# Rotary embedding on half the channels: from 2 MB tiles with 16 KB rows to 4 MB tiles with 32 KB rows, and another way to the tables

## The chip, the cores and the metric

The kernel runs on one core of a Trainium2 chip; the other cores are idle. The metric is the device time of one execution in microseconds (us), given as the median of several. Lower is better. A 'span' is the part of that time that the profiler records; here it is about 1.9 us shorter than the time. Sizes in MB follow the profile (33.55 MB is the whole of `x`); a '2 MB' tile has 2,097,152 bytes.

## The reference

```python
batch, seq, heads, dim = 16, 512, 16, 64          # x: float32, cos and sin: (512, 32)
x1, x2 = x[..., :32], x[..., 32:]
first  = x1[..., :16] * cos[..., :16] - x1[..., 16:] * sin[..., :16]
second = x1[..., :16] * sin[..., :16] + x1[..., 16:] * cos[..., :16]
out = concatenate([first, second, x2], axis=-1)
```

The second half of the channels only passes through. All of `x` (33.55 MB) is read and all of `out` is written, 67 MB in total, and there is little arithmetic for each byte.

## The kernel before

One batch entry is one tile: 512 sequence rows over 128 partitions, four rows per partition. Four rows of 16 heads x 64 floats are 16 KB, contiguous in memory. Loads go out on the sync queue (SP in the profile), stores on the scalar queue (ACT). VectorE (DVE) works in place on the tile. GpSimd (POOL) copies the two tables out to full size first.

```python
K = S // P                                  # 4 rows per partition: runs of 16 KB
xf = x.rearrange("b (p k) h d -> b p (k h d)", p=P)
x_pool = ctx.enter_context(tc.tile_pool(name="xp", bufs=6))
ab_pool = ctx.enter_context(tc.tile_pool(name="abp", bufs=4))
nc.gpsimd.dma_start(out=cosL[:], in_=cosf)
nc.gpsimd.dma_start(out=sinL[:], in_=sinf)
for k in range(K):                          # tables written out over heads and both halves
    nc.gpsimd.tensor_copy(out=dst_c, in_=src_c)
    nc.gpsimd.tensor_copy(out=dst_s, in_=src_s)
for b in range(B):                          # 16 tiles of 2 MB
    x_t = x_pool.tile([P, K, H, D], fp32)
    nc.sync.dma_start(out=x_t..., in_=xf[b])
    nc.vector.tensor_mul(out=a_t[:], in0=x12, in1=cc_op)      # 128 x 2048
    nc.vector.tensor_mul(out=b_t[:], in0=x12, in1=ss_op)
    nc.vector.tensor_tensor(out=x12[:, :, 0:Q], ..., op=subtract)   # 128 x 1024
    nc.vector.tensor_tensor(out=x12[:, :, Q:2*Q], ..., op=add)
    nc.scalar.dma_start(out=of[b], in_=x_t...)
```

## Time and profile before

| | before |
|---|---|
| time | 163.36 us median of 4 (163.12 to 163.46) |
| span | 161.4 us |
| bytes moved | 67.25 MB |
| VectorE busy | 67% |
| DMA, 50 to 141 us | 431 GB/s |

These are lines of the profile page of the kernel before. In the slices each digit is the busy share of 1/40 of the span, in tenths. A queue's line gives its packets, its MB and its share of the 16 DMA engines' time; q1 carries the loads, q10 the stores, q0 the tables. A line that begins with L64 stands for all instructions of line 64 of the kernel: output and inputs with their sizes, how many, then busy us and mean ns of one, then how long the engine was idle before them and what ended most of that wait.

```profile
span 161.4 us, 189 instructions
DVE 108.7 (67%) x64; POOL 6.0 (4%) x14
DMA  5999999999999999999999999999999999999994
...
q1 hardware_dynamic: 2304, 33.56, 49.4%
q10 hardware_dynamic: 2304, 33.56, 48.5%
q0 software_dynamic: 64, 0.13, 0.2%
...
L64 DVE TENSOR_TENSOR a_t<-x_t,CCX 128x2048 f32<-128x2048 f32 x16 | 37.0, 2313 | 42.1 <-DMA x_t<-in_x_dram 30.1
L66 DVE TENSOR_TENSOR x_t<-a_t,b_t 128x1024 f32<-128x1024 f32 x16 | 19.5, 1220 | 0.2
```

The DMA row is full from the second slice to the next to last, and the two tile queues fill 98% of the engines' time. VectorE is idle for a third of the span. It waits for loads; the loads themselves are late because the engines are full.

The table of stretches for the kernel before (start:end, length, busy time of DVE and of POOL with the number of instructions, clock, DMA share, GB/s) says it with a rate:

```profile
12.00:50.00 38.00, 37.83 (x22) 0.47 (x1) 1.00 1.01 426
50.00:141.00 91.00, 61.67 (x37) 0.00 (x0) 1.00 1.01 431
141.00:151.00 10.00, 9.12 (x6) 0.00 (x0) 1.00 1.01 434
151.00:161.40 10.40, 0.00 (x0) 0.00 (x0) 1.00 0.78 336
```

The next line is from the waits of the SP queue before (us in total, number of waits, the longest).

```profile
SPq L57 <- DMA out_dram<-x_t: 107.8, 10, 24.1
```

The load queue waits 107.8 us for stores to free a buffer. That looks like a shortage of buffers, but the engines never run empty meanwhile, and loads that were issued earlier are still moving: in the packet records the load queue has no gap longer than 0.2 us. So this wait costs nothing here.

### The profile page before, as it was taken

How to read it: one execution, taken by the hardware profiler on the slowest of the kernel's cores; microseconds unless marked ns; L12 is line 12 of the kernel's file. 1: busy time of each engine (PE TensorE's matmuls, PEld its weight loads, DVE VectorE, ACT ScalarE, POOL GpSimd, SP SyncE). 2: the span in 40 equal slices, each digit the busy share in tenths (PEclk: the TensorE clock that was granted, in tenths of full speed). 3: DMA queues.
4: the chain of work that ended last, by engine and by line, in shares of the span. 5: the costliest groups of instructions: out<-in, count | busy, mean ns of one | idle time of the engine just before them, and what ended most of it. 6: DMA issues, size and time to landing. Idle time of an engine off the chain costs nothing.

```text
span 161.4 us, 189 instructions
## 1 busy us (share of the span) xinstructions
DVE 108.7 (67%) x64; POOL 6.0 (4%) x14
## 2 busy tenths in 40 slices
DVE  0009999999995692947839296592957939389400
POOL 3090000000000000000000000000000000000000
DMA  5999999999999999999999999999999999999994
GB/s 162 430 414 447 414 382 443 414 430 447 418 434 434 422 443 430 418 451 422 426 443 422 430 434 430 434 434 418 447 422 426 451 414 428 439 422 438 430 422 195
DMA packets 4673, 67.25 MB, mean 417 GB/s; under 512 B 544, under 2 KB 544, under 8 KB 576
## 3 DMA queue, kind: packets, MB, share of 16 engines
q1 hardware_dynamic: 2304, 33.56, 49.4%
q10 hardware_dynamic: 2304, 33.56, 48.5%
q0 software_dynamic: 64, 0.13, 0.2%
q14 instruction: 1, 0.01, 0.0%
HBM read 33.69 MB, written 33.55 MB: 417 GB/s over the span
## 4 chain that ended last, share of the span: by engine, by line
DMA 60%; DVE 28%; POOL 2%; issue 2%; DVEq 1%; POOLq 0%; SPq 0%; PEldq 0%
DMA out_dram<-x_t 31%; DMA x_t<-in_x_dram 25%; DVE a_t L64 9%; DVE b_t L65 8%; DVE x_t L66 6%; DVE x_t L72 5%; DMA cosL<-in_cos_dram 4%; POOL CCX L49 1%; DVEq L105 1%; POOL SSX L50 1%; POOLq L105 0%; SPq L57 0%; DVEq L66 0%; PEldq L105 0%
## 5 line engine op out<-in xcount | busy, mean ns | idle before, releaser
L64 DVE TENSOR_TENSOR a_t<-x_t,CCX 128x2048 f32<-128x2048 f32 x16 | 37.0, 2313 | 42.1 <-DMA x_t<-in_x_dram 30.1
L65 DVE TENSOR_TENSOR b_t<-x_t,SSX 128x2048 f32<-128x2048 f32 x16 | 36.5, 2283 | 0.0
L66 DVE TENSOR_TENSOR x_t<-a_t,b_t 128x1024 f32<-128x1024 f32 x16 | 19.5, 1220 | 0.2
L72 DVE TENSOR_TENSOR x_t<-a_t,b_t 128x1024 f32<-128x1024 f32 x16 | 19.5, 1218 | 0.0
L49 POOL COPY CCX<-cosL 128x512 f32<-128x512 f32 x4 | 2.4, 612 | 5.4 <-DMA cosL<-in_cos_dram 5.4
L50 POOL COPY SSX<-sinL 128x512 f32<-128x512 f32 x4 | 2.4, 614 | 0.1
L39 POOL DMA_DIRECT2D cosL<-in_cos_dram x1 | 0.7, 668 | 0.8 <-PEq L105 0.8
L40 POOL DMA_DIRECT2D sinL<-in_sin_dram x1 | 0.5, 534 | 0.0
L94 POOL MEMSET const-float32-0.0<- 128x1 f32 x1 | 0.1, 98 | 0.2 <-issue 0.2
L94 POOL MEMSET const-bfloat16-1.0<- 128x1 bf16 x1 | 0.1, 101 | 0.0
L94 POOL MEMSET const-uint8-127<- 128x1 uint8 x1 | 0.1, 101 | 0.0
L94 POOL MEMSET const-float32-1.0<- 128x1 f32 x1 | 0.1, 98 | 0.0
## 6 DMA issues: line engine op xcount, KB each, us to landing
x_t<-in_x_dram SPq DMA_DIRECT2D x16, 2048.0 KB, 20.3
out_dram<-x_t ACTq DMA_DIRECT2D x16, 2048.0 KB, 23.4
cosL<-in_cos_dram POOLq DMA_DIRECT2D x1, 64.0 KB, 6.6
sinL<-in_sin_dram POOLq DMA_DIRECT2D x1, 64.0 KB, 7.1
```

Source lines behind the costliest of these rows:

```text
L39: nc.gpsimd.dma_start(out=cosL[:], in_=cosf)
L40: nc.gpsimd.dma_start(out=sinL[:], in_=sinf)
L49: nc.gpsimd.tensor_copy(out=dst_c, in_=src_c)
L50: nc.gpsimd.tensor_copy(out=dst_s, in_=src_s)
L64: nc.vector.tensor_mul(out=a_t[:], in0=x12, in1=cc_op)
L65: nc.vector.tensor_mul(out=b_t[:], in0=x12, in1=ss_op)
L66: nc.vector.tensor_tensor(out=x12[:, :, 0:Q], in0=a_t[:, :, 0:Q], in1=b_t[:, :, Q : 2 * Q], op=mybir.AluOpType.subtract,)
L72: nc.vector.tensor_tensor(out=x12[:, :, Q : 2 * Q], in0=a_t[:, :, Q : 2 * Q], in1=b_t[:, :, 0:Q], op=mybir.AluOpType.add,)
L94: nc = _bacc.Bacc("TRN2", target_bir_lowering=False, num_devices=1)
L105: with _tile.TileContext(nc) as tc:
```

## The change

The intent is larger transfers: eight rows per partition, so 32 KB runs and 4 MB tiles, eight tiles instead of sixteen, five buffers. A partition then holds eight consecutive rows, and two batch entries share a tile. The 512 rows of each table fill only 64 partitions, eight rows each; they are loaded there, and VectorE copies them into both halves of a 128-partition table. The tables are not written out over heads; the multiplies read them with a broadcast instead.

```diff
-    K = S // P
+    K = 8
+    T = B * S // (P * K)          # 8 tiles
+    PB = S // K                   # 64 partitions hold all table rows
...
-    x_pool = ctx.enter_context(tc.tile_pool(name="xp", bufs=6))
-    ab_pool = ctx.enter_context(tc.tile_pool(name="abp", bufs=4))
-    nc.gpsimd.dma_start(out=cosL[:], in_=cosf)
-    nc.gpsimd.dma_start(out=sinL[:], in_=sinf)
-    for k in range(K):  ... nc.gpsimd.tensor_copy x2
+    x_pool = ctx.enter_context(tc.tile_pool(name="xp", bufs=5))
+    ab_pool = ctx.enter_context(tc.tile_pool(name="abp", bufs=1))
+    stage = const_pool.tile([PB, 2, K, HF], fp32)
+    nc.scalar.dma_start(out=stage[:, 0]..., in_=cosf)
+    nc.scalar.dma_start(out=stage[:, 1]..., in_=sinf)
+    table = const_pool.tile([P, 2, K, 2, Q], fp32)
+    for r in range(2):
+        for t in range(2):
+            nc.vector.tensor_copy(out=table[r * PB : (r + 1) * PB, t], in_=stage[:, t, :, 0:Q]...broadcast)
...
+    for t in range(T):
+        nc.sync.dma_start(out=x_t..., in_=xf[t])          # 4 MB, 32 KB runs
+        for k0 in (0, 4):                                 # same VectorE shapes as before
+            ... two multiplies, subtract, add
+        nc.scalar.dma_start(out=of[t], in_=x_t...)
```

More of the change, by code (lines that the diff above doesn't have):

```diff
@@ L20 @@
     fp32 = mybir.dt.float32
+    P = 128
     B, S, H, D = x.shape
@@ L24 @@
     HF = D // 2
-    P = 128
-    K = S // P
-    xf = x.rearrange("b (p k) h d -> b p (k h d)", p=P)
-    of = out.rearrange("b (p k) h d -> b p (k h d)", p=P)
-    cosf = cos.rearrange("(p k) j -> p (k j)", p=P)
-    sinf = sin.rearrange("(p k) j -> p (k j)", p=P)
-    const_pool = ctx.enter_context(tc.tile_pool(name="const", bufs=1))
-    x_pool = ctx.enter_context(tc.tile_pool(name="xp", bufs=6))
-    ab_pool = ctx.enter_context(tc.tile_pool(name="abp", bufs=4))
-    cosL = const_pool.tile([P, K, HF], fp32)
@@ L38 @@
-    sinL = const_pool.tile([P, K, HF], fp32)
-    nc.gpsimd.dma_start(out=cosL[:], in_=cosf)
-    nc.gpsimd.dma_start(out=sinL[:], in_=sinf)
-    CCX = const_pool.tile([P, K, H, 2, Q], fp32)
-    SSX = const_pool.tile([P, K, H, 2, Q], fp32)
-    for k in range(K):
-        dst_c = CCX[:, k].rearrange("p h c j -> p (h c) j")
-        dst_s = SSX[:, k].rearrange("p h c j -> p (h c) j")
-        src_c = cosL[:, k : k + 1, 0:Q].to_broadcast((P, 2 * H, Q))
-        src_s = sinL[:, k : k + 1, 0:Q].to_broadcast((P, 2 * H, Q))
-        nc.gpsimd.tensor_copy(out=dst_c, in_=src_c)
-        nc.gpsimd.tensor_copy(out=dst_s, in_=src_s)
@@ L52 @@
-    cc_op = CCX.rearrange("p k h c j -> p (k h) (c j)")
-    ss_op = SSX.rearrange("p k h c j -> p (k h) (c j)")
-    for b in range(B):
-        x_t = x_pool.tile([P, K, H, D], fp32)
-        nc.sync.dma_start(out=x_t.rearrange("p k h d -> p (k h d)"), in_=xf[b])
-        a_t = ab_pool.tile([P, K * H, HF], fp32)
-        b_t = ab_pool.tile([P, K * H, HF], fp32)
-        x12 = x_t.rearrange("p k h d -> p (k h) d")[:, :, 0:HF]
-        nc.vector.tensor_mul(out=a_t[:], in0=x12, in1=cc_op)
-        nc.vector.tensor_mul(out=b_t[:], in0=x12, in1=ss_op)
-        nc.vector.tensor_tensor(
-            out=x12[:, :, 0:Q],
-            in0=a_t[:, :, 0:Q],
-            in1=b_t[:, :, Q : 2 * Q],
-            op=mybir.AluOpType.subtract,
-        )
-        nc.vector.tensor_tensor(
-            out=x12[:, :, Q : 2 * Q],
-            in0=a_t[:, :, Q : 2 * Q],
-            in1=b_t[:, :, 0:Q],
-            op=mybir.AluOpType.add,
-        )
-        nc.scalar.dma_start(out=of[b], in_=x_t.rearrange("p k h d -> p (k h d)"))
+    K = 8
@@ new lines @@
+    T = B * S // (P * K)
+    PB = S // K
+    REP = P // PB
+    xf = x.rearrange("b s h d -> (b s h d)").rearrange("(t p f) -> t p f", t=T, p=P)
+    of = out.rearrange("b s h d -> (b s h d)").rearrange("(t p f) -> t p f", t=T, p=P)
+    cosf = cos.rearrange("(p k) j -> p (k j)", k=K)
+    sinf = sin.rearrange("(p k) j -> p (k j)", k=K)
+    const_pool = ctx.enter_context(tc.tile_pool(name="const", bufs=1))
+    x_pool = ctx.enter_context(tc.tile_pool(name="xp", bufs=5))
+    ab_pool = ctx.enter_context(tc.tile_pool(name="abp", bufs=1))
@@ new lines @@
+    stage = const_pool.tile([PB, 2, K, HF], fp32)
+    nc.scalar.dma_start(out=stage[:, 0].rearrange("p k j -> p (k j)"), in_=cosf)
+    nc.scalar.dma_start(out=stage[:, 1].rearrange("p k j -> p (k j)"), in_=sinf)
+    table = const_pool.tile([P, 2, K, 2, Q], fp32)
+    for r in range(REP):
+        for t in range(2):
+            nc.vector.tensor_copy(
+                out=table[r * PB : (r + 1) * PB, t],
+                in_=stage[:, t, :, 0:Q].unsqueeze(2).to_broadcast((PB, K, 2, Q)),
+            )
@@ new lines @@
+    C = table[:, 0].rearrange("p k c j -> p k (c j)")
+    Sn = table[:, 1].rearrange("p k c j -> p k (c j)")
+    KC = 4
+    for t in range(T):
+        x_t = x_pool.tile([P, K, H, D], fp32)
+        nc.sync.dma_start(out=x_t.rearrange("p k h d -> p (k h d)"), in_=xf[t])
+        for k0 in range(0, K, KC):
+            x1 = x_t[:, k0 : k0 + KC, :, 0:HF]
+            c = C[:, k0 : k0 + KC].unsqueeze(2).to_broadcast((P, KC, H, HF))
+            s = Sn[:, k0 : k0 + KC].unsqueeze(2).to_broadcast((P, KC, H, HF))
+            a_t = ab_pool.tile([P, KC, H, HF], fp32)
+            b_t = ab_pool.tile([P, KC, H, HF], fp32)
+            nc.vector.tensor_mul(out=a_t[:], in0=x1, in1=c)
+            nc.vector.tensor_mul(out=b_t[:], in0=x1, in1=s)
+            nc.vector.tensor_sub(
+                out=x1[:, :, :, 0:Q], in0=a_t[:, :, :, 0:Q], in1=b_t[:, :, :, Q:HF]
+            )
+            nc.vector.tensor_add(
+                out=x1[:, :, :, Q:HF], in0=a_t[:, :, :, Q:HF], in1=b_t[:, :, :, 0:Q]
+            )
+        nc.scalar.dma_start(out=of[t], in_=x_t.rearrange("p k h d -> p (k h d)"))
```

## The prediction

> **What bounds the kernel now.** The DMA engines. The page's slices show them at 9 tenths in every slice between the first and last; the table of stretches gives 431 GB/s from 50 to 141 us. The Trainium skill, "DMA: Bandwidth & Descriptors", section "Where 436 GB/s comes from", gives a ceiling of 435; this trace is 1% under it. The packet records show it directly: each tile row is one 16,384-byte packet taking 0.611 us, 4,096 of them over 16 engines, 156.4 us of the 161.4 us span. The first packet starts about 2.9 us in; then the engines have no gap, and the last packet ends with the span. VectorE is 67% busy; its 30.1 us of waiting for loads (the waits view) cost nothing. The load queue waits 107.8 us for stores to free buffers; that too is only two queues sharing full engines.
>
> **What the change does.** Bytes stay at 67 MB.
>
> 1. Rows become 32,768 bytes. Two packet sizes of this trace (4,096 bytes in 0.159 us, 16,384 in 0.611) give about 27.2 GB/s per engine plus 8 ns per packet. If a 32 KB row stays one packet, it should take about 1.214 us, and 128 per engine 155.3 us: 1.1 us less. If it is cut at 16 KB, nothing changes. Half as many completion packets (9 ns each) save about 0.15 us.
> 2. Tables: the 8 Pool copies (5.5 us in all) go; 2 loads of 64 KB on the scalar queue and 4 VectorE copies of 64x256 come in. Estimate: 0.2 to 0.3 us a copy, from the skill's "VectorE: DVE Perf Modes", errata table (no VectorE copy in this trace to check it). The table packets alternate with 32 KB packets of loads, so tables may land at 12 to 20 us instead of 7.8. The first 4 MB tile lands at about 14 us anyway (2 MB: about 9.8). VectorE starts at 14 to 20 us instead of 11.95.
> 3. VectorE work per byte is unchanged: 128x2048 multiplies of 2.29 us, 128x1024 at 1.22. Single scratch buffers add waits between them; I estimate 6.8 to 7.1 us per 2 MB, 13.6 to 14.2 per tile. VectorE stays under 75% busy.
> 4. Five tiles of 4 MB allow 20 MB of loads in flight (was 12): engines are fed for 49 us before they need a store; the first store is ready at 28 to 34 us.
> 5. The end is coarser: the last tile takes 14 us to compute and its store 9.7. Following both queues by arithmetic: the last load lands near 130, its compute ends near 144, while the store before it runs until 148. So the engines don't run dry; slack about 3 us. VectorE starting later than about 26 us would use it up.
>
> **On the critical path:** only the DMA stream. Gain 0 to 1.2 us; possible loss 0 to 2 us in the tail. Predicted 162.6 us, range 161.0 to 165.0 (span about 160.7). Faster by over 2%: 0.04; within: 0.87; slower: 0.09.
>
> **What would show it.** Right: about 1,024 data packets per queue, each near 1.21 us; DMA slices 9 throughout; 431 to 434 GB/s in the middle; no gap before the last store. Wrong in step 1: still 2,304 packets per queue. Wrong in step 5: a DMA slice under 9 near 145 us and a slower total. Wrong in step 2: VectorE's first multiply after 26 us.
>
> **What would make it wrong:** 32 KB rows placing the engines' streams on the same memory banks, lowering the rate; uneven engines, so that a 4 MB tile lands late; tables starved behind large packets.

## The result, and the profile after

| | before | after |
|---|---|---|
| time, median of 4 | 163.36 us | 162.34 us (162.22 to 162.40) |
| span | 161.4 us | 160.4 us |
| packets on q1, q10 | 2,304, 2,304 | 1,152, 1,312 |
| VectorE's first multiply | 11.95 us | 18.29 us |
| DMA, 50 to 141 us | 431 GB/s | 432 GB/s |

The ratio is 0.9936, with a 95% interval from 0.9922 to 0.995. A ratio here is the mean time of one kernel's runs over that of the other's runs of the same rounds, so it is not quite the ratio of the medians. Executions over 1.5% slower than the fastest of the same kernel are left out of the means. The change is real, but it is 0.6%: within 2%.

The same lines of the page after:

```profile
span 160.4 us, 155 instructions
DVE 110.8 (69%) x68; POOL 0.2 (0%) x4
DMA  7999999999999999999999999999999999999993
...
q1 hardware_dynamic: 1152, 33.55, 49.3%
q10 hardware_dynamic: 1312, 33.69, 48.7%
...
L65 DVE TENSOR_TENSOR a_t<-x_t,table 128x2048 f32<-128x2048 f32 x16 | 36.7, 2292 | 13.6 <-DMA x_t<-in_x_dram 13.2
L48 DVE COPY table<-stage 64x256 f32<-64x256 f32 x4 | 1.1, 287 | 17.1 <-DMA stage<-in_cos_dram 12.2
```

The DMA row is still full. The packets halved: 1,152 on q1 are 1,024 runs of 32 KB and 128 completion packets. VectorE does the same work at the same speed, and starts later because it waits for the tables. The start in order of time, from the timeline after (start, length, engine, line):

```profile
12.19 0.59 DVE L48 COPY table<-stage 64x256 f32<-64x256 f32 x2 [12.19 <-DMA stage<-in_cos_dram]
17.67 0.59 DVE L48 COPY table<-stage 64x256 f32<-64x256 f32 x2 [4.90 <-DMA stage<-in_sin_dram]
18.29 2.29 DVE L65 TENSOR_TENSOR a_t<-x_t,table 128x2048 f32<-128x2048 f32 x1
```

And the stretches after:

```profile
12.00:50.00 38.00, 32.58 (x22) 0.00 (x0) 1.00 1.01 429
50.00:141.00 91.00, 77.12 (x47) 0.00 (x0) 1.00 1.00 432
141.00:151.00 10.00, 1.11 (x1) 0.00 (x0) 1.00 0.98 423
151.00:160.40 9.40, 0.00 (x0) 0.00 (x0) 1.00 0.78 335
```

The trace also records every DMA packet. This table is worked out from those records (times on the span's own clock; 'period' is the steady time in which 2 MB are loaded and 2 MB stored, from the completions of the stores):

```
                                   before     after
one data packet, us (median)       0.611      1.213     (16,384 and 32,768 bytes)
data packets per engine            256        128
period for 2 MB in + 2 MB out, us  9.7246     9.6814
first packet, us                   1.75       1.73
last packet ends, us               160.16     159.20
empty engines in between, us       1.07       0.83      (mean over the 16 engines)
```

Sixteen periods make up the 33.55 MB in each direction: 16 x (9.7246 - 9.6814) = 0.69 us. The packets' window shrank by 158.41 - 157.47 = 0.94 us. The rest is not settled. The two edges, where the engines start and stop at slightly different moments, have 0.24 us less of empty engines. Where the stores begin, 23 packets of the kernel before were slow (up to 1.12 us instead of 0.611, 0.4 us per engine in all), and none of the changed kernel, which had 16 slow ones where its tables arrive (0.2 us). All of this share beside the 0.69 us was counted, not tested. Empty engines come to between 0.73 and 1.42 us in the runs with 8 and 16 KB packets below, so their 0.24 us can't be put down to the packets.

The Trainium skill, "DMA: Bandwidth & Descriptors", section "Where 436 GB/s comes from", puts the ceiling at 435 GB/s. The period after is 8,388,608 bytes in 19.363 us, 433.2 GB/s; before it was 431.3. So little was left to gain.

### The profile page after: what moved, and what is told of

It reads as the page before. It is cut to its first block, busy times and chain, and to the rows that moved or that the text cites. A ratio compares the mean times of both kernels' runs of the same rounds, so it can differ in the third digit from the quotient of the medians.

```text
span 160.4 us, 155 instructions
## 1 busy us (share of the span) xinstructions
DVE 110.8 (69%) x68; POOL 0.2 (0%) x4
## 3 DMA queue, kind: packets, MB, share of 16 engines
q1 hardware_dynamic: 1152, 33.55, 49.3%
q10 hardware_dynamic: 1312, 33.69, 48.7%
HBM read 33.69 MB, written 33.55 MB: 419 GB/s over the span
## 4 chain that ended last, share of the span: by engine, by line
DMA 53%; DVE 30%; issue 4%; DVEq 1%; ACTq 0%; SPq 0%
DMA x_t<-in_x_dram 21%; DMA out_dram<-x_t 21%; DVE b_t L66 11%; DMA stage<-in_sin_dram 10%; DVE a_t L65 10%; DVE x_t L70 5%; DVE x_t L67 4%; DVEq L99 1%; ACTq L41 0%; DVE table L48 0%; SPq L58 0%; DVEq L65 0%
## 5 line engine op out<-in xcount | busy, mean ns | idle before, releaser
L65 DVE TENSOR_TENSOR a_t<-x_t,table 128x2048 f32<-128x2048 f32 x16 | 36.7, 2292 | 13.6 <-DMA x_t<-in_x_dram 13.2
L66 DVE TENSOR_TENSOR b_t<-x_t,table 128x2048 f32<-128x2048 f32 x16 | 36.5, 2284 | 0.0
L48 DVE COPY table<-stage 64x256 f32<-64x256 f32 x4 | 1.1, 287 | 17.1 <-DMA stage<-in_cos_dram 12.2
```

What stands on the lines that cost most here:

```text
L48: nc.vector.tensor_copy(out=table[r * PB : (r + 1) * PB, t], in_=stage[:, t, :, 0:Q].unsqueeze(2).to_broadcast((PB, K, 2, Q)),)
L65: nc.vector.tensor_mul(out=a_t[:], in0=x1, in1=c)
L66: nc.vector.tensor_mul(out=b_t[:], in0=x1, in1=s)
```

## The experiments

Theory A: the DMA stream bounds both kernels, and the gain is the cost of each packet, so only the length of a contiguous run matters. Rival B: the new path of the tables made it. Rival C: larger DMAs and more bytes in flight made it. All runs below gave correct results. Kernels of one group ran on one chip beside the kernel before, whose medians there were 163.20, 163.25 and 163.26 us. Ratios are to the kernel before.

### Runs cut to 16 KB (r16) and to 8 KB (r8)

```diff
-        nc.sync.dma_start(out=x_t[...all rows...], in_=xf[t])
+        for r0 in range(0, K, RW):        # RW = 4 (16 KB) or 2 (8 KB); stores likewise
+            nc.sync.dma_start(out=x_t[:, r0 : r0 + RW]..., in_=xf[t][:, lo:hi])
```

> The changed kernel with every load and store of a 4 MB tile issued as two, each with 16 KB runs; tiles, buffers, tables and VectorE work stay. Theory A (the gain is the cost per packet): packets of 0.611 us again, 4,096 of them, and the steady stretch again moves 4 MB in 9.725 us instead of 9.681, so about 0.7 to 0.9 us slower than the changed kernel: 163.0 to 163.3 us, the time of the kernel before. Rival B (the gain is the tables' new path or the earlier start) and rival C (the gain is the larger tile and the 20 MB of loads in flight): both are kept here, so 162.3 us.

> As the run with 16 KB runs, but four DMAs with 8 KB runs each. Theory A: 8,192 data packets of about 0.310 us; the line through the 16 KB and 32 KB streams gives about 5.4 ns per packet and engine, 256 packets more than with 16 KB, so 1.4 us more: 164.5 us; by the packets' own durations (8 ns each) up to 165.5. Rivals B and C: 162.3 us.

Measured: 163.09 us for 16 KB, ratio 0.9991 (0.9977 to 1.0004), and 164.40 us for 8 KB, ratio 1.007 (1.0058 to 1.0082). The queue lines of the 16 KB run's page and then of the 8 KB run's:

```profile
q1 hardware_dynamic: 2304, 33.56, 49.3%
q10 hardware_dynamic: 2464, 33.69, 48.8%
```

```profile
q1 hardware_dynamic: 4608, 33.56, 49.7%
q10 hardware_dynamic: 4768, 33.69, 49.2%
```

With the packets of the kernel before, the time of the kernel before is back, although tile size, buffers and tables are the changed ones. The periods fall on a line:

```
run     packets per engine in a period     period, us (2 MB in + 2 MB out)
8 KB    32                                 9.812
16 KB   16                                 9.7246    (16 packets fewer: 0.087 us less, 5.5 ns each)
32 KB    8                                 9.6814    ( 8 packets fewer: 0.043 us less, 5.4 ns each)
```

Each packet costs about 5.4 ns of an engine beside its bytes, its share of the completions included. Drawn on to no packets at all, the line ends at 9.638 us, or 435.2 GB/s: an estimate from these three periods, and the ceiling that the page cited above gives. The rivals expected 162.3 us in both runs and are out as the whole cause. But these runs halved the bytes per DMA together with the run, so one question was left for the next run.

### One DMA of 4 MB with two 16 KB runs per partition (b2)

```diff
+    xf = x.rearrange("(t c) (p k) h d -> t p c (k h d)", c=2, p=P)   # 4 rows of each of two sequences
-        nc.sync.dma_start(out=x_t.rearrange("p k h d -> p (k h d)"), in_=xf[t])
+        nc.sync.dma_start(out=x_t.rearrange("p (c k) h d -> p c (k h d)", c=2), in_=xf[t])
```

The tables follow the new rows, on 128 partitions; stores are cut the same way.

> The changed kernel with one 4 MB DMA per tile as before, but each partition filled with two runs of 16 KB (four rows of each of two sequences) in place of one of 32 KB. It parts the run's length from the bytes per DMA, which the two cut runs changed together. Theory A (cost per packet): 4,096 packets of 0.611 us, 4 MB of the mixed stream in 9.72 us, 163.0 to 163.3 us. Rival C (bytes per DMA, fewer completions): 162.3 us.

Measured: 163.21 us, ratio 0.9998 (0.998 to 1.0015). The run's q1 line:

```profile
q1 hardware_dynamic: 2176, 33.55, 49.5%
```

That is 2,048 data packets and 128 completions: long DMAs with short runs. The gain is gone, so it belongs to the run, not to the DMA. The packet records give the share: once only stores are left, 4 MB take 9.725 us as two DMAs with 16 KB runs, 9.719 as one DMA with 16 KB runs, and 9.681 as one DMA with 32 KB runs. The DMA's size is 6 ns of those 44. The periods are better evidence than the total here, since this run also had slow packets where its stores begin (1.0 us per engine).

### Whole 32 KB runs, 64 partitions per DMA (half64)

```diff
+        for p0 in (0, 64):
+            nc.sync.dma_start(out=x_t[p0 : p0 + 64]..., in_=xf[t][p0 : p0 + 64])
```

> The changed kernel with every load and store issued as two DMAs of 64 partitions each, so 2 MB per DMA as in the kernel before, but runs of 32 KB. Theory A (packets): 2,048 data packets of 1.213 us as in the changed kernel, completion packets doubled: 162.3 to 162.6 us. Rival C (bytes per DMA): 163.3 us, as before. A third possibility, from the Trainium skill, SBUF page, section on the DMA port swizzle: partitions 0 to 63 reach only 8 of 16 ports, so if loads of one half are alone in flight the rate there falls to about half; then packets get up to twice as long in the load-only first 49 us and the time rises by far over 2%.

Measured: 238.44 us; the two runs counted as fast are at 233 and 235, and the profiled run (239.07 us) counts as slow, being over 1.5% above them. This is over 40% slower than before (ratio 1.4325). Stretches of this run, the first two with loads alone in flight, the third with loads and stores:

```profile
0.00:12.00 12.00, 0.00 (x0) 0.20 (x4) 1.00 0.85 180
12.00:47.00 35.00, 17.60 (x14) 0.00 (x0) 1.00 1.01 212
...
100.00:141.00 41.00, 25.48 (x16) 0.00 (x0) 1.00 1.00 334
```

The engines look 100% busy at half the rate: a busy share of 1.01 can hide a stream at 212 GB/s, so read GB/s beside it. A run of 32 KB takes 2.084 us in the median of the loads instead of 1.213. The Trainium skill, "SBUF — State Buffer", section "Door 1: The DMA port swizzle", says that partitions 0 to 63 reach only 8 of 16 ports, about 218 GB/s; the 212 here agrees. As a test of rival C the run says nothing, because the ports swamp what it was made for; the run with two 16 KB runs per partition did that job.

### 64 KB runs (k16)

```diff
-    K = 8            # xp bufs=5, KC = 4, one store per tile
+    K = 16           # xp bufs=3, KC = 2, two stores per tile, 32 KB runs each
```

The staging of the tables shares the scratch tile, so that it fits.

> A try at going further: 16 rows per partition, four tiles of 8 MB loaded with 64 KB runs, three buffers; stores stay at 32 KB runs, each issued when its half tile is done; scratch halved to fit. Theory A: if a 64 KB run is one packet, about 2.418 us each, 64 packets fewer per engine, 0.35 us less, if the engines never run dry: 162.0 us. My queue arithmetic has them just not run dry, with little slack (VectorE can start only near 24 us); if they do, some us slower. If a 64 KB run is cut in two, nothing is gained: 162.3 us at best.

Measured: 164.08 us, ratio 1.0053 (1.0035 to 1.0071): slower than before. A 64 KB run is one packet of 2.419 us, as expected, and the sum of all packets' time is 157.6 us per engine against 157.2 in the changed kernel: the saving on packets is eaten by slow ones. The main loss is at the end. The first engine finishes the last store at 158.97 us and the last engine at 161.72, while in the changed kernel these are 158.27 and 159.20. The stretches of this run show it (last figures: DMA share and GB/s):

```profile
141.00:159.00 18.00, 7.24 (x8) 0.00 (x0) 1.00 0.96 411
159.00:163.00 4.00, 0.00 (x0) 0.00 (x0) 1.00 0.08 33
```

This was the try at beating both kernels, and it failed. It changed the tiles and buffers together with the run, and its load queue had no packet from 72.3 to 86.9 us, so it does not show that 64 KB runs are worse.

### The new tables in the old tiling (before_newtab)

```diff
 (kernel before: K = 4, 16 tiles, 6 buffers)
-    nc.gpsimd.dma_start(...) x2 ; 8 gpsimd copies to CCX, SSX
+    nc.scalar.dma_start(...) x2 ; 2 vector copies to table; multiplies read it with a broadcast over heads
```

> The kernel before (2 MB tiles, 16 KB runs, six buffers) with the tables taken the changed way: loaded on the scalar queue, copied on VectorE, broadcast over heads. Theory A: the tables are off the critical path, so 163.2 us, as the kernel before, though VectorE starts earlier or later by some us. Rival B (the tables' path made the gain): 162.3 us.

Measured: 163.02 us, ratio 0.9984 (0.9968 to 1.0). VectorE starts at 13.98 us here, against 11.95 before. The centre is 0.16% of the change's 0.64%, and the interval reaches from 0.32% to nothing. The runs with 16 KB runs above have the new tables too, and their ratios, 0.9991 and 0.9998, show next to no gain. The period here is 9.725 us, as before. So rival B is not the main cause; whether the tables give nothing or a few tenths of a microsecond outside the steady stretch stays open.

### The tables ahead of the tiles (tabfirst)

```diff
-    nc.scalar.dma_start(out=stage[:, 0]..., in_=cosf)      # and sin
+    nc.sync.dma_start(out=stage[:, 0]..., in_=cosf)        # and sin, so before the first tile
```

> The changed kernel with its two table loads issued on the sync queue ahead of the tiles, so that their small packets no longer alternate with 32 KB packets: tables should land by 5 us in place of 18.5, and VectorE start near 15 us (first tile) in place of 18.3. Theory A: nothing waits for VectorE, so 162.3 us (within 0.2). A rival in which the late start costs: up to 3 us faster, 159 to 161 us.

Measured: 163.98 us, ratio 1.0042 (1.0026 to 1.0058), so 1.6 us slower than the changed kernel's 162.34. Both expectations missed. Its timeline:

```profile
1.32 0.58 SPq L42 DMA_DIRECT2D stage<-in_sin_dram  x1
1.95 2.71 SPq L58 DMA_DIRECT2D x_t<-in_x_dram  x5
2.89 0.59 DVE L48 COPY table<-stage 64x256 f32<-64x256 f32 x2 [2.89 <-DMA stage<-in_cos_dram]
...
14.61 2.29 DVE L65 TENSOR_TENSOR a_t<-x_t,table 128x2048 f32<-128x2048 f32 x1 [10.37 <-DMA x_t<-in_x_dram]
```

The tables did arrive early and VectorE did start at 14.6 us, and none of it helped. What hurt is the second line: the sync queue issues its first tile at 1.95 us instead of 0.73, because issuing two small DMAs took its time. The first tile packet starts at 3.17 us instead of 1.73. The first stretch of this run, and then that of the changed kernel:

```profile
0.00:4.00 4.00, 0.91 (x4) 0.20 (x4) 1.00 0.52 147
```

```profile
0.00:4.00 4.00, 0.00 (x0) 0.20 (x4) 1.00 0.75 254
```

In the first 4 us this run's engines are busy for 0.52 of the time, and the changed kernel's for 0.75. Here a stream that is full from then on carries the loss at its start through to its end: the 1.44 us of late start are most of the 1.8 us by which this run's span is longer.

### VectorE starting late (late4 and late9)

```diff
+    junk = const_pool.tile([P, 1536], fp32)
+    for _ in range(4):        # 9 in the other run
+        nc.vector.tensor_add(out=junk[:], in0=..table.., in1=..table..)
```

> The changed kernel with four idle additions on VectorE ahead of the first tile (7 us; its first multiply at about 25 us instead of 18.3). The queue arithmetic has slack until about 31 us: 162.3 us, within 0.2. If the late start costs at all in proportion: up to 169 us.

> The changed kernel with nine idle additions on VectorE (about 1.76 us each, 15.8 us in all) ahead of the first tile, so its first multiply is at about 34 us. Theory A with the queue arithmetic: the slack of the late start ends near 31 us, because then the eight tiles run on VectorE without a pause and the last store is issued too late; about 3 us of empty DMA engines before the last store, 165 us. If VectorE were on the critical path throughout: 178 us. If there were no limit: 162.3 us.

Measured: 164.91 us with four additions (ratio 1.0113, 1.0086 to 1.0139) and 164.66 us with nine (ratio 1.0084, 1.0065 to 1.0103). The first multiply is at 25.15 us with four. With nine the compiler's order put two of the additions among the first tile's steps, so its first multiply is at 30.77; the first half tile is done when the expectation had it. The larger delay came out near its 165 us, but not in the way I had written. There is no gap before the last store, so the number came near by luck; the engines are empty for 0.7 us near 62 us, when the first store is done and the second not yet under way, and the rest is slow packets (158.80 us per engine against 157.17 in the changed kernel). The smaller delay missed: no cost was expected, and it cost 2.6 us, no less than the 2.3 us of the larger one.

The stretches of the run with four additions, and then those of the changed kernel:

```profile
60.00:80.00 20.00, 19.82 (x12) 0.00 (x0) 1.00 1.01 410
80.00:141.00 61.00, 54.32 (x33) 0.00 (x0) 1.00 1.00 432
...
159.00:162.80 3.80, 0.00 (x0) 0.00 (x0) 1.00 0.16 69
```

```profile
60.00:80.00 20.00, 19.82 (x12) 0.00 (x0) 1.00 1.02 439
80.00:141.00 61.00, 47.44 (x29) 0.00 (x0) 1.00 1.00 431
```

From 60 to 80 us the late run moves 410 GB/s instead of 439, at a full busy share. The packet records say what happens there. A load may go out only when a store has freed a buffer. With VectorE late the first store lands late, the sixth load is issued at 62.73 us instead of 55.29, and the load queue has no packet at any engine from 61.8 to 66.7 us. The engines still have stores, so they count as busy. From 65.8 to 77.8 us some 35 packets of both queues are slow (over 1.3 and up to 2.35 us instead of 1.21); the packets' time per engine comes to 158.44 us against 157.17, and the engines end apart: 158.62 us for the first and 161.55 for the last, against 158.27 and 159.20. These two together are the whole loss of about 2.4 us of span. The last store is not later for it: it is issued at 142.07 us, and at 142.14 in the changed kernel. In the changed kernel the load queue never runs dry (its longest gap is 1.8 us). That the dry queue causes the slow packets is argued from their order in time, not shown, and how long it is dry does not set the loss: 15.5 us with nine additions cost no more than 4.8 us with four, and the run with four buffers, next, was dry for 8.2 us without such a loss.

### Four and three buffers (bufs4, bufs3)

```diff
-    x_pool = ctx.enter_context(tc.tile_pool(name="xp", bufs=5))
+    x_pool = ctx.enter_context(tc.tile_pool(name="xp", bufs=4))   # and 3
```

> The changed kernel with four 4 MB buffers in place of five. Theory A with the queue arithmetic: the load ring is fed for 39 us, the last load lands 8.5 us later (near 137 instead of 128), and the last store is issued about when the one before it ends: no slack is left, 0 to 1 us of empty engines, 162.3 to 163.3 us. If the fifth buffer itself made the gain (rival C): clearly above 163.3 us.

> The changed kernel with three 4 MB buffers. The queue arithmetic: the engines run empty from 34 to 37 us, again near 47, and about 8 us before the last store, 14 us in all: 176 us. If only bytes count: 162.3 us.

Measured: 162.86 us with four, ratio 0.9973 (0.9949 to 0.9997), and 176.61 us with three, ratio 1.0821 (1.0796 to 1.0846). Both times fell where the queue arithmetic put them. With four, the load queue runs dry from 48.6 to 56.8 us in the packet records, yet only 16 packets are slow afterwards (up to 1.80 us). The run is half a microsecond slower than with five, and what fits that is the end, as expected: the last store is issued at 149.05 us, when the one before it is ending, and the engines are empty for 0.7 us. Two stretches of the run with three buffers:

```profile
50.00:150.00 100.00, 65.19 (x40) 0.00 (x0) 1.00 1.00 429
150.00:166.00 16.00, 12.82 (x8) 0.00 (x0) 1.00 0.32 137
```

The middle streams at full rate; then all but one tile has been stored, and the engines wait for VectorE to finish the last one. Of the 14 us of empty engines that were expected, 10.6 came before this last store (8 expected) and 1.7 near 43 us (3 and more expected between 34 and 47). Three buffers of 4 MB hold the bytes of the six buffers of 2 MB before, and yet cost 13 us. With tiles twice as large, the wait for the last tile's arithmetic is twice as long, and the number of tiles in the pipeline half. For rival C: four buffers of 4 MB keep the steady period (19.36 us for 4 MB each way), so the fifth is not what shortens it; but of the gain of 1.0 us they keep only 0.4.

### More work on VectorE (slowdve)

```diff
+            nc.vector.tensor_mul(out=b_t[:], in0=x1, in1=s)  # the same again
```

> The changed kernel with the second multiply of every chunk done twice: about 2.2 us more per chunk, 18.3 us per tile in place of 13.85, VectorE about 146 us in all. The queue arithmetic: the DMA engines take 4 MB in and 4 MB out in 19.4 us, so the middle still hides it, but after the loads end VectorE hands over a tile only every 18.3 us and the engines wait for the last stores; first multiply at 18.3, end of VectorE near 164.5, then one store of about 12 us: 178 to 179 us. A theory in which VectorE is hidden as long as it is below 100% busy: 162.3 us.

Measured: 179.90 us, ratio 1.1021 (1.0999 to 1.1043), about one microsecond over the expected range. VectorE is 83% busy. The stretches:

```profile
0.00:130.00 130.00, 111.85 (x65) 0.20 (x4) 1.00 0.99 423
...
141.00:150.00 9.00, 8.90 (x6) 0.00 (x0) 1.00 0.27 117
...
159.00:168.00 9.00, 6.97 (x5) 0.00 (x0) 1.00 0.14 58
```

For 130 us the DMA stream hides VectorE. When the loads are done, a store needs only 9.7 us for 4 MB, VectorE needs 18.5 us per tile (18.3 expected), and the engines wait twice, 8.5 us each time. VectorE can set the time though it is far below 100% busy.

## Why the prediction was right

The prediction was 162.6 us, and 162.34 us was measured, inside its range and within 2% of before. Point by point:

- The bound: right. The runs with other packet lengths move the time, and the new tables alone hardly do.
- Step 1, packets: right in kind, and almost twice too large. A 32 KB run is one packet of 1.213 us (1.214 expected). Adding up durations gave 1.1 us, and 0.15 for completions; the periods give 0.69 us, since the packets of an engine overlap by about 4 ns in the records. The cost per packet is 5.4 ns with all effects, not 8. The measured gain was 1.0 us, and its other 0.3 us is in no step of the prediction; that the total came so near is in part luck.
- Step 2, tables: right. They were usable at 12.2 and 17.7 us (12 to 20 expected), a copy took 0.287 us (0.2 to 0.3), and VectorE began at 18.29 us (14 to 20).
- Step 3: right. Half a tile takes 25.21 - 18.29 = 6.92 us (6.8 to 7.1).
- Step 4: right. The first store was issued at 32.1 us.
- Step 5, the end: right in that no engine ran empty. The last store was issued at 142.1 us, while the one before it ended only at about 149. The slack was 6.8 us, not 3. The limit 'VectorE starting later than about 26 us' (31 in the later expectations) had the wrong mechanism: a first multiply at 25.15 us already cost 2.6 us, and not at the last store, which went out as before. I had counted only when all engines are empty. The loss came with slow packets after the load queue had run dry; what makes them slow stays open.
- One reading was off: I lined the packets up with the end of the span, and so had the first at 2.9 us. On the span's clock they run from 1.75 to 160.16 us. Nothing else in the sum depended on it.

The named risks (memory banks, uneven engines, starved tables) did not show in the changed kernel: the middle ran at 432 GB/s, the engines ended within 0.9 us of each other, and the tables came within the expected time. Uneven engines did show in the runs with 64 KB runs and with the late start.

## What to carry to other kernels

When the DMA engines are full from end to end, cost a change per packet and per byte, and count what it does at the start of the stream. Where the tables sat and when VectorE began hardly mattered here, up to a first multiply at 18.29 us; at 25.15 us it cost 2.6 us. Longer contiguous runs paid, but from 8 to 32 KB each doubling gave under 1%, and larger tiles need more bytes of buffer to be safe: three 4 MB buffers lost 8% where six 2 MB buffers kept the engines full. Don't let a small load go ahead of the first large one on its queue. Look in the packet records for a queue that runs dry and for slow packets after it, since the busy share shows neither.

## What the Trainium skill lacked or had wrong

- "DMA: Bandwidth & Descriptors" gives rates by bytes per DMA and names a fixed overhead per packet for small descriptors, but has no trn2 measurement of the run's length above 4 KB: 9.812, 9.7246 and 9.6814 us per 2 MB in and 2 MB out for 8, 16 and 32 KB, 5.4 ns per packet and engine. The bytes per DMA made 6 ns of 44 here.
- The same page, in the note on 436 and 360 GB/s, and "SBUF — State Buffer", in its summary, name about 358 GB/s, in those two places, as what binds transfers between HBM and SBUF. With one core running, 431 to 433 GB/s were measured. "HBM Reference" has this right for a core alone.
- "SBUF — State Buffer", section "Can I just issue two DMAs to hit both halves?", says that it gains almost nothing. For loads alone that holds (212 GB/s). It does not say that loads and stores on two queues at once do better: 334 GB/s in the same run.
- "VectorE: DVE Perf Modes", errata table: 58 + FD/2 cycles give 0.194 us for the 64x256 fp32 copy at 0.96 GHz; measured 0.287. The fixed term of about 150 cycles that the page adds below the table gives 0.290.
- No page that I read treats a load queue that runs dry while stores keep the engines busy. With four additions 2.4 us of span were lost after 4.8 dry us, in slow packets (up to 2.35 us instead of 1.21) and engines that end 2.9 us apart instead of 0.9; with four buffers 8.2 dry us had no such loss.
